# Loads of the dense expert stage moved to ScalarE's queue, its start reordered, and an index row moved to PSUM

## The chip, the cores and the metric

The kernel runs on one core of one Trainium2 chip. The metric is device time in microseconds (us). TensorE (PE in the profile, its weight loads PEld) multiplies matrices into PSUM, VectorE (DVE), ScalarE (ACT) and GpSimd (POOL) compute beside it, and SyncE (SP) issues most DMAs. ACT and POOL issue DMAs too, in the order of their own programs.

## What is computed

The input is 512 tokens of width 1024. A first block mixes gated linear attention with sparse latent attention. Then comes the expert layer, which this change touches, and after it a second block (pooling, stick-breaking attention). The expert layer, cut to what matters:

```python
q = (h @ w_q).reshape(B, S, 8, 256)
s1 = einsum('bshd,nd->bshn', q[..., :128], sub_keys_1)
s2 = einsum('bshd,nd->bshn', q[..., 128:], sub_keys_2)
v1, i1 = top_k(s1, 16);  v2, i2 = top_k(s2, 16)
best, ci = top_k(all 256 sums v1 + v2, 16)
expert_idx = i1[ci // 16] * 128 + i2[ci % 16]      # 128 x 128 experts
gates = softmax(best)
a = gelu(einsum('td,thkd->thk', h, expert_u[expert_idx])) * gates
out = einsum('thk,thkd->td', a, expert_v[expert_idx])
```

## The kernel before, in words

The program is a list of items, each of which issues a few instructions on several engines; every engine then runs its own instructions in that order. All products are float32, made of three passes (L366 to L368): the operands are split into a rounded high part (ACT, L424 for weights) and a rest (mostly POOL, L425). Weights pass through `raw`, which has room for two loads of 1 MB.

**The key stage** (`peer_keys`) finds the 16 experts of each token and head. DVE does most of it. `number` compares a row of the indices 0 to 49 (`c50`, an SBUF row) with the chosen positions (L1322), POOL multiplies by the expert numbers (L1324), DVE sums (L1330). `soft` (L1377 to L1379) makes the gates, `turn` transposes numbers (L1386) and gates (L1387) on PE.

**The table stage** (`peer_table`) builds, for the first 384 tokens, a dense table of gates, expert by token, from small outer products (L1435), and writes it to DRAM (`gates`).

**Hidden products.** For these 384 tokens the layer is computed densely, over all 128 chunks of 128 experts. Chunk c's hidden product is h times its 128 columns of u: 24 matmuls of 384 columns. 72 of the chunks are computed early, in the key and table stages, to keep PE busy there; they are copied out (L1480) and written to DRAM (`hidden`). These chunks are called **spilled** here, and the other 56, computed in the dense stage, **fresh**.

**The dense stage** goes over 32 groups of four chunks. `gate_chunk` takes a chunk: ACT applies GELU (L1519 on the PSUM bank of a fresh chunk, L1516 from the reloaded buffer of a spilled one), DVE multiplies with the gates (L1523, three per chunk), ACT rounds (L1528), DVE subtracts for the rest (L1530). From four chunks, eight **out blocks** of 12 matmuls each (`peer_out`) are made, each of which DVE adds to its accumulator (L1562). A group has four positions, in the order of its chunks 0, 2, 1, 3; usually 0 and 1 are spilled, and 2 and 3 fresh. At each position a chunk is gated, and two out blocks of the group before run on PE. Groups 0, 6, 13, 19 and 26 have four spilled chunks.

In between, the last 128 tokens are computed sparsely: POOL gathers expert rows (L1589), DVE multiplies and adds them (L1617, the dot; L1606, the add), about one per position, and one more in every third group.

The gates of a group (three loads of 256 KB) and the spilled products (192 KB each) are loaded by `fetch_gates`, called by `gate_chunk` with a look-ahead of three chunks, on SP's queue, between the weight loads. A weight load waits until POOL has finished with the `raw` buffer that it takes.

PSUM has eight banks. In the dense stage two pairs hold the sparse rows. Chunks and out blocks take turns through the other four, the ring `out=[0,1,6,7]`, whose banks appear as `bank0_69`, `bank1_70`, `bank6_71` and `bank7_72` below.

The lines of the changed functions follow.

Of the kernel before, what the change touches and what calls it, by code (L numbers as in the profile page):

```python
# [18 lines left out]
P = 128  # L19
# [4 lines left out]
ND = NT - P  # L24
# [6 lines left out]
W = 32  # L31
# [278 lines left out]
class K:  # L310
# [927 lines left out]
    def peer_keys(self):  # L1238

        nc, A = self.nc, self.A  # L1240
# [3 lines left out]
        def keys(u):  # L1244
            A.new_wide("plain")
            A.plain.wake(8 * D)
            self.rows = A.plain.alloc(8 * D, high=False, name="rows")
            self.sk = A.alloc(256, name="sk")
            nc.vector.tensor_copy(self.sk.v(256), u.raw.v(256))
            self.E = A.alloc(NT, name="E")  # L1250
            self.best = A.alloc(NT, name="best")
            self.c50 = A.alloc(64, name="c50")
            nc.gpsimd.iota(self.c50.v(50), pattern=[[1, 50]], base=0, channel_multiplier=0,
                           allow_small_or_imprecise_dtypes=True)

        def ev_q(b, ps):
            s = st[b // 2]
# [60 lines left out]
        def number(h, t):  # L1318

            s = st[h]  # L1320
            eq = A.wide.alloc(800, name="eq")
            nc.vector.tensor_tensor(eq.v(16, 50), self.c50.v(50)[:, None, :].to_broadcast([P, 16, 50]),  # L1322
                                    s["J"].v(TB, 16)[:, t, :, None].to_broadcast([P, 16, 50]), op=OP.is_equal)
            nc.gpsimd.tensor_mul(eq.v(16, 50), eq.v(16, 50), s["X"].v(TB, 50)[:, t, None, :].to_broadcast([P, 16, 50]))  # L1324
            s.setdefault("eq", []).append(eq)
            if t == TB - 1:
                self.free(s["X"], s["J"])
# [5 lines left out]
        items = [Item(keys, [uk], 0.0)]  # L1333
        q = self.blocks("wq", self.t["w_q"], 16, lambda: self.h2, ev_q)
# [34 lines left out]
    def peer_gates(self):  # L1369

        nc, A = self.nc, self.A

        def soft():
            g = self.best.v(32, 16)
            nc.scalar.activation(self.best.v(NT), self.best.v(NT), AF.Exp)
            z = self.tmp(32)
            nc.vector.reduce_sum(z.v(32), g, axis=AX.X)  # L1377
            nc.vector.reciprocal(z.v(32), z.v(32))
            nc.vector.tensor_tensor(g, g, z.v(32)[:, :, None].to_broadcast([P, 32, 16]), op=OP.mult)  # L1379
            self.free(z, self.c50, self.sk)  # L1380

        def turn():
            pe, pg = self.bank("att"), self.bank("att")
            for t in range(TB - 1):
                c = slice(t * P, t * P + P)
                nc.tensor.transpose(pe[:, c], self.E.v(NT)[:, c], self.ident)  # L1386
                nc.tensor.transpose(pg[:, c], self.best.v(NT)[:, c], self.ident)  # L1387
            self.gT, self.iaT, self.ibT = [A.alloc(ND, high=False, name="gT") for _ in range(3)]
            nc.scalar.copy(self.gT.v(ND), pg[:, :ND])
            ei, e2 = self.tmp(ND), self.tmp(ND)  # L1390
            nc.vector.tensor_copy(ei.v(ND, dt=I32), pe[:, :ND])
            nc.vector.tensor_scalar(e2.v(ND, dt=I32), ei.v(ND, dt=I32), P - 1, None, op0=OP.bitwise_and)
# [12 lines left out]

    def peer_table(self, first, fill):
# [43 lines left out]
        items = []  # L1450
        lag = 4
        for n in range(ND // 4 + lag):
            def fn(n=n):
                if n >= lag:
                    outer(n - lag)
                if n < ND // 4:
                    quad(n)
            items.append(Item(fn, (), 0.9))
            if n == lag - 1:
                items += first  # L1460
            if n >= lag and (n - lag) % 4 == 3 and n < ND // 4:
                items += fill[:1]
                del fill[:1]
        return items + fill

    def peer_hidden(self, chunks, spill):

        nc = self.nc
        items = []
        for c0 in chunks[::2]:  # L1470
            u = Unit(self.t["u"][c0 // 2], 2 * D, uses=2, name="u")
            for j in range(2):
                def fn(w, c=c0 + j, j=j):
                    ps = self.bank("hid" if spill else "out")[:, :ND]
                    for k in range(KB):
                        s = slice(j * D + k * P, j * D + k * P + P)
                        self.mm3(ps, (w.hi[:, s], w.lo[:, s]), (self.h2.hi[:, k, slice(ND)], self.h2.lo[:, k, slice(ND)]), k == 0, k == KB - 1)
                    if spill:
                        g = self.rows.v(ND, at=6 * D + self.spilled[c] % 5 * ND)
                        nc.scalar.copy(g, ps)  # L1480
                        self.load(self.H[self.spilled[c]], g, nc.scalar)
                    else:
                        self.gate_chunk(c, ps)
                    if c == P - 1:
                        self.h2.free()
                items.append(Item(fn, [u], 5.3))
        return items

    def fetch_gates(self, upto):

        while self.q_next < min((upto + 3) // 4, P // 4):
            c = 4 * self.q_next
            slots = [self.A.slot("plain", NT, "gates") for _ in range(3)]
            for q, b in enumerate(slots):
                n = P // W
                self.load(b.v(n, 4 * W), self.G[:, n * q:n * q + n, c:c + 4].rearrange("p g b t -> p g (b t)"))
            self.g_slots[self.q_next] = [slots, 4]
            self.q_next += 1
        while self.g_next < min(upto, P):
            c = self.order[self.g_next]  # L1500
            hb = None
            if c in self.spilled:
                hb = self.tmp(ND)
                self.load(hb.v(ND), self.H[self.spilled[c]])
            self.g_bufs[c] = hb
            self.g_next += 1

    def gate_chunk(self, c, ps=None):

        nc = self.nc  # L1510
        i = self.order.index(c)
        self.fetch_gates(i + 3)
        hb = self.g_bufs.pop(c)
        if ps is None:
            ps = self.bank("out")[:, :ND]
# [124 lines left out]
    def peer(self, table, late):  # L1640
# [6 lines left out]
        self.spilled = {c: i for i, c in enumerate(ahead)}  # L1647
        self.order = []
        for gi in range(groups):
            self.order += [4 * gi + i for i in ((0, 2, 1, 3) if gi else range(4))]  # L1650
        rows = self.dram.tile([P, P * ND + 1024], F32, name="gates")
        self.G = rows[:, :P * ND].rearrange("p (g b t) -> p g b t", b=P, t=W)
        self.H = self.dram.tile([len(ahead), P, ND], F32, name="hidden")
# [8 lines left out]
        def reload():  # L1662
            self.x2 = FRows(self, KB, name="x2", slots=True)
            for i in range(KB):
# [6 lines left out]
        items += turn + self.peer_table(hid[n1 - 2:n1], hid[n1:])  # L1671
        end = len(items) - 5
        items[end:end] = [self.rings_at(hid=[6, 7], out=[0, 1, 6, 7]), Item(self.rows_banks, (), 0.0),
                          Item(lambda: self.fetch_gates(5), (), 0.0)]
        items.append(Item(begin, (), 0.0))
        rest = dict(zip(fresh, self.peer_hidden(fresh, False)))
        items.append(rest[6])
        for c in range(3):
            items.append(Item(lambda c=c: (self.gate_chunk(c), self.lowers()), (), 0.0))
        sparse = self.peer_rows()  # L1680
        out = self.peer_out()
        pend = []
        for gi in range(groups):
# [5 lines left out]
            for i in range(4):  # L1689
                c = self.order[4 * gi + i]  # L1690
                n = 1 if gi else 0
                now, sparse = sparse[:n], sparse[n:]
                add, dot = [a for a, _ in now], [b for _, b in now]
                mine = [rest[c] if c in rest else Item(lambda c=c: self.gate_chunk(c), (), 0.0)] if c > 2 and c != 6 else []
                items += add + mine if c in rest else mine + add
                items += (dot or [Item(self.lowers, (), 0.0)]) + pend[2 * i:2 * i + 2]
                if i == 1 and gi and gi % 3 == 0:
                    items += sparse[0]
                    sparse = sparse[1:]
# [422 lines left out]
    def build(self):  # L2122
# [22 lines left out]
        seq.append(self.split_by(nc.vector))  # L2145
        seq.append(self.rings_at(proj=[0, 1, 2, 3], att=[4, 5, 6, 7], hid=[4, 5], out=[0, 1, 2, 3], misc=[6]))
        seq += self.merge()
        seq.append(self.rings_at(proj=[0, 1], att=[2, 3, 4, 5], hid=[6, 7], out=[0, 1, 2, 3]))
        seq.append(self.split_by(nc.gpsimd))
        seq += self.peer(28, 6)  # L2150
        pool = self.pool()
        seq += pool[:2] + [self.split_by(nc.gpsimd)] + pool[2:]
        seq += self.stick()
# [91 lines left out]
```

## Time and profile before

| what | value |
|---|---|
| median of 3 runs | 2877.93 us (2876.39 to 2881.17) |
| the profiled execution | 2877.26 us, span 2875.5 us |
| PE busy | 2700.3 us, 94% of the span |
| DVE, POOL, ACT busy | 64%, 56%, 44% |
| mean granted TensorE clock | 0.978 |

Read the table as averages over stages with different limits. The profile counts a matmul as busy until its modelled end, so the idle time before a matmul and the granted clock of a stretch say more than the share. A granted clock of 1.00 is 2.4 GHz; in the stretches below 1.00 it was at 1.2 GHz for a part of the time. In a row of a timeline, the bracket at the end holds the idle time before the instruction and what ended it.

### The profile page before, as it was taken

The page shows a single profiled execution, that of the slowest core. Times are in us where ns is not written, and L with a number is a line of the kernel's source. Part 1 is how long each engine was busy: PE and PEld are TensorE (multiplying, and loading weights), DVE is VectorE, ACT ScalarE, POOL GpSimd, SP SyncE. Part 2 cuts the span into 40 slices and gives each one's busy share as a digit, 9 for nine tenths or more (in the row PEclk, how much of TensorE's full clock was granted, in tenths as well). Part 3 has the DMA queues.
Part 4 walks back from the last instruction along what each step waited for, and adds up shares of the span by engine and source line. Part 5 has one row for each costly group of instructions (what it writes and reads, how often), then busy time and mean ns, then how long its engine had stood idle before and what let it go on. Part 6 is the DMA issues. An engine that isn't in the chain of part 4 may idle for free.

```text
span 2875.5 us, 40315 instructions
## 1 busy us (share of the span) xinstructions
PE 2700.3 (94%) x14510; PEld 2434.8 (85%) x14510; DVE 1843.2 (64%) x3826; ACT 1254.6 (44%) x2508; POOL 1605.2 (56%) x1481
## 2 busy tenths in 40 slices
PE   5999999898999899898998989989999999999997
PEld 3897788776999899898998989989888887888896
DVE  7334576677888888377767776776585532544655
ACT  4443525523333376444443443444443234445543
POOL 4000234304888765466766766767655554766774
PEclk9999999999999899999999999999999999999998
DMA  6221221265443456598898999888323232221210
GB/s 231 103 74 59 77 89 41 90 227 183 146 142 130 182 227 237 207 334 328 318 333 316 339 330 330 328 321 300 124 87 117 88 103 74 74 74 59 74 59 30
DMA packets 138649, 502.21 MB, mean 175 GB/s; under 512 B 11472, under 2 KB 79184, under 8 KB 89296
## 3 DMA queue, kind: packets, MB, share of 16 engines
q1 hardware_dynamic: 106272, 321.81, 32.8%
q0 software_dynamic: 19072, 136.32, 11.6%
q10 hardware_dynamic: 13104, 41.49, 3.6%
q8 instruction: 114, 1.87, 0.3%
q14 instruction: 87, 0.71, 0.1%
HBM read 456.06 MB, written 43.52 MB: 174 GB/s over the span
## 4 chain that ended last, share of the span: by engine, by line
PE 36%; DVE 7%; DMA 7%; issue 3%; ACT 3%; POOL 3%; SPq 1%; DVEq 0%; POOLq 0%; ACTq 0%
PE bank L366 12%; PE bank L367 11%; PE bank L368 11%; DMA slot<-hidden 5%; POOL split L425 2%; DVE bank L1606 2%; DMA plain<-in_uv_dram,slot 2%; DVE bank L1523 1%; DVE plain L1617 1%; PE bank L2020 1%; DVE slot L1562 1%; PE bank L2019 1%; SPq L376 1%; ACT split L424 1%; ACT bank L1516 0%
## 5 line engine op out<-in xcount | busy, mean ns | idle before, releaser
L425 POOL TENSOR_TENSOR split<-raw,split 128x512 fp32r<-128x512 f32 x832 | 1074.2, 1325 | 637.0 <-ACT split L424 579.0
L366 PE MATMUL bank<-slot,split 128*128 128x384 f32 (+2 forms) x1932 | 706.6, 366 | 16.4 <-DVE slot L373 5.1
L367 PE MATMUL bank<-slot,split 128*128 128x384 f32 (+2 forms) x1932 | 700.8, 363 | 0.5 <-DVE slot L373 0.5
L368 PE MATMUL bank<-slot,split 128*128 128x384 f32 (+2 forms) x1932 | 700.2, 362 | 0.3 <-POOL split L425 0.3
L366 PE MATMUL bank<-wide,split 128*128 128x384 f32 (+1 forms) x1688 | 621.6, 368 | 80.8 <-DVE wide L1530 56.7
L367 PE MATMUL bank<-wide,split 128*128 128x384 f32 (+1 forms) x1688 | 610.8, 362 | 10.0 <-POOL wide L612 10.0
L368 PE MATMUL bank<-wide,split 128*128 128x384 f32 (+1 forms) x1688 | 609.6, 361 | 0.0
L424 ACT CAST split<-raw 128x512 fp32r<-128x512 f32 x953 | 522.3, 619 | 105.4 <-PE bank L367 60.8
L366 PEld LDWEIGHTS bank<-wide,split 128*128 128x128 f32 x1688 | 323.4, 192 | 130.1 <-DVE wide L1530 70.9
L366 PEld LDWEIGHTS bank<-slot,split 128*128 128x128 f32 (+1 forms) x1932 | 366.1, 189 | 59.9 <-DVE slot L373 6.2
L367 PEld LDWEIGHTS bank<-slot,split 128*128 128x128 f32 (+1 forms) x1932 | 365.8, 189 | 37.2 <-DVE slot L373 1.7
L368 PEld LDWEIGHTS bank<-slot,split 128*128 128x128 f32 (+1 forms) x1932 | 365.4, 189 | 37.5 <-POOL split L425 0.6
L367 PEld LDWEIGHTS bank<-wide,split 128*128 128x128 f32 x1688 | 323.7, 192 | 39.6 <-POOL wide L612 12.5
L368 PEld LDWEIGHTS bank<-wide,split 128*128 128x128 f32 x1688 | 323.2, 191 | 26.3
L1523 DVE TENSOR_TENSOR bank<-bank,slot 128x128 f32<-128x128 f32 x384 | 114.5, 298 | 211.0 <-ACT bank L1516 125.6
L1589 POOL DMA_INDIRECT plain<-in_uv_dram,slot x128 | 121.4, 949 | 130.6 <-DVE bank L1606 103.5
L1617 DVE SCALAR_TENSOR_TENSOR plain<-plain,bank 128x1024 f32<-128x1024 f32 x128 | 155.2, 1213 | 24.4 <-DMA plain<-in_uv_dram,slot 24.4
L1606 DVE SCALAR_TENSOR_TENSOR bank<-plain,slot,bank 128x1024 f32<-128x1024 f32 x127 | 162.5, 1280 | 0.0
L1528 ACT CAST wide<-bank 128x384 fp32r<-128x384 f32 x128 | 61.4, 480 | 212.5 <-DVE bank L1523 209.2
L425 DVE TENSOR_TENSOR split<-raw,split 128x512 fp32r<-128x512 f32 x121 | 82.1, 740 | 98.5 <-ACT split L424 96.5
L1562 DVE TENSOR_TENSOR slot<-slot,bank 128x384 f32<-128x384 f32 x240 | 122.5, 548 | 2.5 <-PE bank L368 2.5
L2007 POOL TENSOR_TENSOR slot<-plain,slot 128x384 fp32r<-128x384 f32 (+3 forms) x125 | 107.6, 891 | 0.4 <-DVE slot L2004 0.4
(355 smaller groups left out, 3835.0 us busy)
## 6 DMA issues: line engine op xcount, KB each, us to landing
raw<-in_u_dram SPq DMA_DIRECT2D x64, 1024.0 KB, 5.0
raw<-in_v_dram SPq DMA_DIRECT2D x64, 1024.0 KB, 5.0
gates<-wide ACTq DMA_DIRECT2D x12, 2048.0 KB, 7.8
slot<-gates SPq DMA_DIRECT2D x96, 256.0 KB, 9.0
plain<-in_w_ada_dram SPq DMA_DIRECT2D x32, 512.0 KB, 6.4
raw<-in_w_pool_dram SPq DMA_DIRECT2D x16, 1024.0 KB, 4.9
hidden<-plain ACTq DMA_DIRECT2D x72, 192.0 KB, 2.9
slot<-hidden SPq DMA_DIRECT2D x72, 192.0 KB, 8.1
```

The lines of the kernel that those rows point to most:

```text
L366: mm(out, lhsT=w[0], rhs=x[0], start=start, stop=False, skip_group_check=True)
L367: mm(out, lhsT=w[0], rhs=x[1], start=False, stop=False, skip_group_check=True)
L368: mm(out, lhsT=w[1], rhs=x[0], start=False, stop=stop, skip_group_check=True)
L424: self.nc.scalar.copy(u.hl.hi[:, c], u.raw.v(u.n)[:, c])
L425: (u.lo or self.lo_engine).tensor_sub(u.hl.lo[:, c], u.raw.v(u.n)[:, c], u.hl.hi[:, c])
L1523: nc.vector.tensor_mul(p, p, b.v(P // W, 4, W)[:, :, c % 4])
L1528: nc.scalar.copy(a.hi, ps)
L1562: nc.vector.tensor_add(acc, acc, ps)
L1589: self.nc.gpsimd.indirect_dma_start(out=self.uvs[k % 4].rearrange("p a b -> p (a b)"), out_offset=None, in_=self.t["uv"], in_offset=bass.I ...
L1606: nc.vector.scalar_tensor_tensor(acc, v, a, acc, op0=OP.mult, op1=OP.add)
L1617: nc.vector.scalar_tensor_tensor(u, u, 1.0, self.hx, op0=OP.mult, op1=OP.mult, accum_out=self.dx.v(P)[:, k:k + 1])
L2007: nc.gpsimd.tensor_sub(out[i].lo, e.v(NT - i * P), out[i].hi)
```

## The change

1. `fetch_gates` issues the loads on ACT's queue, except those of the first two groups of gates and the first four spilled chunks. The look-ahead for chunks is 4 in place of 3; that for the gates stays.
2. The dense stage starts in another order: the hidden product of chunk 6, the first fresh one, is computed into bank 6 as before the rest, but chunks 0 to 3 are gated ahead of it, and group 1 runs in the order 2, 0, 1, 3. From there on the ring is `out=[0,1,7]`.
3. `c50` lies in PSUM, in bank 5 behind the columns that `iota` uses later; the ring of the key stage gives up that bank.
4. Two hidden products more stand in the key stage, and two fewer in the table stage (26 in place of 28, two of the 23 places of the table are skipped).

```diff
+            c = self.tmp(50)
+            nc.gpsimd.iota(c.v(50), ...)
+            self.c50 = self.psum[5][:, 256:306]
+            nc.scalar.copy(self.c50, c.v(50))
...
-            if n >= lag and (n - lag) % 4 == 3 and n < ND // 4:
+            if n >= lag and (n - lag) % 4 == 3 and n < ND // 4 and n - lag not in (27, 59):
...
+                    elif c == 6:
+                        self.early = ps
...
-        while self.q_next < min((upto + 3) // 4, P // 4):
+        while self.q_next < min((upto + 2) // 4, P // 4):
...
-                self.load(b.v(n, 4 * W), self.G[...])
+                self.load(b.v(n, 4 * W), self.G[...], nc.scalar if self.q_next > 1 else nc.sync)
...
-                self.load(hb.v(ND), self.H[self.spilled[c]])
+                self.load(hb.v(ND), self.H[self.spilled[c]], nc.scalar if self.g_next > 4 else nc.sync)
...
-        self.fetch_gates(i + 3)
+        self.fetch_gates(i + 4)
...
-            self.order += [4 * gi + i for i in ((0, 2, 1, 3) if gi else range(4))]
+            self.order += [4 * gi + i for i in ((0, 2, 1, 3) if gi > 1 else (2, 0, 1, 3) if gi else range(4))]
...
-        items.append(rest[6])
-        for c in range(3):
+        items += [self.rings_at(out=[6]), rest[6], self.rings_at(out=[0, 1, 7])]
+        for c in range(4):
             items.append(Item(lambda c=c: (self.gate_chunk(c), self.lowers()), (), 0.0))
+        items.append(Item(lambda: (self.gate_chunk(6, self.early), self.lowers()), (), 0.0))
...
-        seq.append(self.rings_at(proj=[0, 1], att=[2, 3, 4, 5], hid=[6, 7], out=[0, 1, 2, 3]))
+        seq.append(self.rings_at(proj=[0, 1], att=[2, 3, 4], hid=[6, 7]))
...
-        seq += self.peer(28, 6)
+        seq += self.peer(26, 6)
```

ACT's program in a group in the middle of the dense stage, before: GELU and rounding of a fresh chunk, two small instructions of the sparse rows, the rounding of weights, and GELU of a spilled chunk.

```order
L1519 ACTIVATE bank7_72<-bank7_72 128x384
L1528 CAST wide694_9365<-bank7_72 128x384
L1613 ACTIVATE slot500_7521<-slot500_7521 128x1
L1614 ACTIVATE slot500_7521<-slot500_7521 128x1
L424 CAST split_66<-raw_65 128x512 x4
L1516 ACTIVATE bank6_71<-slot783_12520 128x384
L1528 CAST wide694_9365<-bank6_71 128x384
```

The same place in the changed kernel, down to the next fresh chunk (its lines 1526, 1535, 1620, 1621 and 1523 are 1519, 1528, 1613, 1614 and 1516 of before):

```order
L1526 ACTIVATE bank0_69<-bank0_69 128x384
L1535 CAST wide694_9366<-bank0_69 128x384
L1620 ACTIVATE slot500_7583<-slot500_7583 128x1
L1621 ACTIVATE slot500_7583<-slot500_7583 128x1
L424 CAST split_66<-raw_65 128x512 x4
L376 DMA slot785_12641<-gates_133 128x4x128
L376 DMA slot786_12642<-gates_133 128x4x128
L376 DMA slot787_12643<-gates_133 128x4x128
L1523 ACTIVATE bank0_69<-slot783_12484 128x384
L1535 CAST wide694_9366<-bank0_69 128x384
...
L376 DMA slot788_12709<-hidden_134 128x384
L1526 ACTIVATE bank0_69<-bank0_69 128x384
```

Once per group three issues of gates stand ahead of the GELU of a spilled chunk; the issue of a spilled product stands ahead of the GELU of a fresh one. All chunks are now gated in bank 0.

DVE's program from the last multiplication of one fresh chunk to the next additions, before; the banks show which of the four each product took.

```order
L1530 TENSOR_TENSOR wide694_9365<-bank7_72,wide694_9365 128x384
L1617 SCALAR_TENSOR_TENSOR plain_67,slot500_7521<-plain_67,bank1024_2_9370 128x1024
L1562 TENSOR_TENSOR slot708_9552<-slot708_9552,bank0_69 128x384
L1562 TENSOR_TENSOR slot709_9553<-slot709_9553,bank1_70 128x384
...
L1530 TENSOR_TENSOR wide694_9365<-bank6_71,wide694_9365 128x384
L1562 TENSOR_TENSOR slot710_9554<-slot710_9554,bank7_72 128x384
L1562 TENSOR_TENSOR slot711_9555<-slot711_9555,bank0_69 128x384
```

The same rows in the changed kernel (1537, 1624 and 1569 are 1530, 1617 and 1562 of before):

```order
L1537 TENSOR_TENSOR wide694_9366<-bank0_69,wide694_9366 128x384
L1624 SCALAR_TENSOR_TENSOR plain_67,slot500_7583<-plain_67,bank1024_2_9371 128x1024
L1569 TENSOR_TENSOR slot708_9553<-slot708_9553,bank1_70 128x384
L1569 TENSOR_TENSOR slot709_9554<-slot709_9554,bank7_72 128x384
...
L1537 TENSOR_TENSOR wide694_9366<-bank0_69,wide694_9366 128x384
L1569 TENSOR_TENSOR slot710_9555<-slot710_9555,bank1_70 128x384
L1569 TENSOR_TENSOR slot711_9556<-slot711_9556,bank7_72 128x384
```

The out blocks take turns in two banks now, 1 and 7, and every chunk stands in bank 0. The order of DVE's instructions is the same.

## Rows read from the trace of the kernel before

**Rows 1.** Stretches: length; busy us (instructions) of PE, PEld, DVE, ACT, POOL; clock; DMA.

```profile
1341.00:1373.00 32.00, 25.21 (x126) 24.25 (x127) 26.23 (x49) 13.62 (x35) 17.86 (x16) 0.89 0.94 351
...
1517.00:1561.00 44.00, 34.66 (x173) 33.38 (x173) 31.04 (x59) 16.28 (x40) 25.64 (x23) 0.88 0.93 347
...
1677.00:1718.00 41.00, 33.34 (x177) 32.06 (x176) 29.32 (x58) 16.37 (x41) 22.62 (x21) 0.92 0.95 349
...
1866.00:1908.00 42.00, 34.33 (x174) 33.69 (x173) 27.96 (x55) 16.29 (x40) 25.23 (x22) 0.88 0.94 339
...
1206.00:1992.00 786.00, 730.15 (x4039) 712.68 (x4039) 566.87 (x1088) 333.27 (x825) 536.68 (x458) 0.97 0.88 322
```

**Rows 2.** Waits from 1206 to 1992: total us, times, longest us.

```profile
ACT bank L1516 <- DMA slot<-hidden: 131.9, 32, 6.0
...
PE bank L366 <- DVE wide L1530: 47.7, 38, 5.4
...
DVE plain L1617 <- DMA plain<-in_uv_dram,slot: 24.4, 19, 2.4
```

**Rows 3.** Timeline, group 13: SP's issues, ACT's GELU, PE's wait.

```profile
1516.17 2.05 SPq L376 DMA_DIRECT2D slot<-gates  x3
1518.26 5.63 SPq L376 DMA_DIRECT2D slot<-hidden  x2
...
1529.05 0.49 ACT L1516 ACTIVATE bank<-slot 128x384 f32<-128x384 f32 x1 [4.70 <-DMA slot<-hidden]
...
1532.25 0.69 PE L366 MATMUL bank<-wide,split 128*128 128x384 f32 x1 [4.13 <-DVE wide L1530]
```

**Rows 4.** Timeline of DVE in a half group without a late load.

```profile
1564.79 1.03 DVE L1562 TENSOR_TENSOR slot<-slot,bank 128x384 f32<-128x384 f32 x2
1566.20 0.97 DVE L1523 TENSOR_TENSOR bank<-bank,slot 128x128 f32<-128x128 f32 x3 [0.38 <-ACT bank L1516]
...
1568.27 0.55 DVE L1530 TENSOR_TENSOR wide<-bank,wide 128x384 fp32r<-128x384 f32 x1
...
1569.87 1.01 DVE L1562 TENSOR_TENSOR slot<-slot,bank 128x384 f32<-128x384 f32 x2
```

**Rows 5.** Same half group: first out-block matmuls, GELU of the spilled chunk.

```profile
1560.91 0.33 PE L366 MATMUL bank<-wide,split 128*128 128x384 f32 x1
...
1565.68 0.49 ACT L1516 ACTIVATE bank<-slot 128x384 f32<-128x384 f32 x1
...
1573.39 0.33 PE L366 MATMUL bank<-wide,split 128*128 128x384 f32 x1
```

**Rows 6.** DMA issues by tile: ns min/median/max, first and last start.

```profile
L376 SPq DMA_DIRECT2D slot<-gates x96: 360/531/2537, 1168.6 to 1997.1; - x96
...
L376 ACTq DMA_DIRECT2D hidden<-plain x72: 326/326/353, 697.1 to 1191.9; - x72
L376 SPq DMA_DIRECT2D slot<-hidden x72: 319/645/8310, 1183.5 to 1981.1; - x72
```

**Rows 7.** DMA from 1206 to 1992: KB each, median us from issue to landing.

```profile
slot<-gates SPq DMA_DIRECT2D x87, 256.0 KB, 9.1
slot<-hidden SPq DMA_DIRECT2D x66, 192.0 KB, 8.2
```

**Rows 8.** Timeline, start of the dense stage.

```profile
1203.93 0.56 DVE L1530 TENSOR_TENSOR wide<-bank,wide 128x384 fp32r<-128x384 f32 x1 [0.60 <-ACT wide L1528]
...
1204.55 0.69 PE L366 MATMUL bank<-wide,split 128*128 128x384 f32 x1 [9.05 <-DVE wide L1530]
```

**Rows 9.** Turn from keys to table: PE's waits.

```profile
963.73 0.47 PE L1386 MATMUL bank<-plain,slot 128*128 128x128 f32 x1 [3.15 <-DVE slot L1330]
...
969.21 0.45 PE L1387 MATMUL bank<-plain,slot 128*128 128x128 f32 x1 [5.01 <-DVE slot L1379]
```

**Rows 10.** DVE comparisons: index row in SBUF (L1322), in PSUM (L1414); ns min/median/max.

```profile
L1322 DVE TENSOR_TENSOR wide<-plain,slot x32: 977/1535/2556, 728.0 to 960.3; 128x800 f32<-128x800 f32 x32
...
L1414 DVE TENSOR_TENSOR slot<-bank,slot x96: 675/681/692, 981.4 to 1156.0; 128x512 f32<-128x512 f32 x96
```

More of the change, by code (lines that the diff above doesn't have):

```diff
@@ L1251, in keys @@
             self.best = A.alloc(NT, name="best")
-            self.c50 = A.alloc(64, name="c50")
-            nc.gpsimd.iota(self.c50.v(50), pattern=[[1, 50]], base=0, channel_multiplier=0,
+            c = self.tmp(50)
+            nc.gpsimd.iota(c.v(50), pattern=[[1, 50]], base=0, channel_multiplier=0,
                            allow_small_or_imprecise_dtypes=True)
+            self.c50 = self.psum[5][:, 256:306]
+            nc.scalar.copy(self.c50, c.v(50))
+            self.free(c)
         def ev_q(b, ps):
@@ L1321, in number @@
             eq = A.wide.alloc(800, name="eq")
-            nc.vector.tensor_tensor(eq.v(16, 50), self.c50.v(50)[:, None, :].to_broadcast([P, 16, 50]),
+            nc.vector.tensor_tensor(eq.v(16, 50), self.c50[:, None, :].to_broadcast([P, 16, 50]),
                                     s["J"].v(TB, 16)[:, t, :, None].to_broadcast([P, 16, 50]), op=OP.is_equal)
@@ L1379, in soft @@
             nc.vector.tensor_tensor(g, g, z.v(32)[:, :, None].to_broadcast([P, 32, 16]), op=OP.mult)
-            self.free(z, self.c50, self.sk)
+            self.free(z, self.sk)
         def turn():
@@ L1489, in fetch_gates @@
     def fetch_gates(self, upto):
-        while self.q_next < min((upto + 3) // 4, P // 4):
+        nc = self.nc
+        while self.q_next < min((upto + 2) // 4, P // 4):
             c = 4 * self.q_next
@@ L1495, in fetch_gates @@
                 n = P // W
-                self.load(b.v(n, 4 * W), self.G[:, n * q:n * q + n, c:c + 4].rearrange("p g b t -> p g (b t)"))
+                self.load(b.v(n, 4 * W), self.G[:, n * q:n * q + n, c:c + 4].rearrange("p g b t -> p g (b t)"),
+                          nc.scalar if self.q_next > 1 else nc.sync)
             self.g_slots[self.q_next] = [slots, 4]
@@ L1673, in peer @@
         items[end:end] = [self.rings_at(hid=[6, 7], out=[0, 1, 6, 7]), Item(self.rows_banks, (), 0.0),
-                          Item(lambda: self.fetch_gates(5), (), 0.0)]
+                          Item(lambda: self.fetch_gates(6), (), 0.0)]
         items.append(Item(begin, (), 0.0))
         rest = dict(zip(fresh, self.peer_hidden(fresh, False)))
-        items.append(rest[6])
-        for c in range(3):
+        items += [self.rings_at(out=[6]), rest[6], self.rings_at(out=[0, 1, 7])]
+        for c in range(4):
             items.append(Item(lambda c=c: (self.gate_chunk(c), self.lowers()), (), 0.0))
+        items.append(Item(lambda: (self.gate_chunk(6, self.early), self.lowers()), (), 0.0))
         sparse = self.peer_rows()
@@ L1693, in peer @@
                 add, dot = [a for a, _ in now], [b for _, b in now]
-                mine = [rest[c] if c in rest else Item(lambda c=c: self.gate_chunk(c), (), 0.0)] if c > 2 and c != 6 else []
+                mine = [rest[c] if c in rest else Item(lambda c=c: self.gate_chunk(c), (), 0.0)] if c > 3 and c != 6 else []
                 items += add + mine if c in rest else mine + add
```

## The prediction

> **What bounds the kernel now.** I read four views, in this order. The waits of the dense stage come first: the longest sum is ACT's, 131.9 us in 32 places, for reloaded spilled products, and PE waits 47.7 us in 38 places for the rest that DVE makes of gated chunks [rows 2]. Then the busy time of stretches: from 1206 to 1992 us PE works 730.15 of 786.00 us, so 55.85 us are idle. The groups with four spilled chunks (6, 13, 19, 26) hold much of it: 159 us with 127.54 busy, so 31.5 us idle, and a clock of 0.88 to 0.92. Length times what is missing to 1.00 (32 x 0.11 + 44 x 0.12 + 41 x 0.08 + 42 x 0.12) gives 17.1 us for the clock, together 48.6 us [rows 1]. The rest of the stage has 24.4 us idle. Then the timeline of group 13 for the cause: SP's issue of three gates takes 2.05 us, that of two spilled products is held for 5.63 us, ACT waits 4.70 us for one of them, and 2.7 us after its GELU ends PE waits 4.13 us [rows 3]. SP issues them between weight loads, each of which waits for its buffer. Last, a half group without a late load: its first out-block matmul stands at 1560.91, the next at 1573.39, 12.48 us for 72 matmuls, 0.173 us each; 24 (a hidden product, or two out blocks) take 4.16 [rows 5]. All times below count from that 1560.91.
>
> **The loads on ACT's queue.** ACT has no weight loads, and the look-ahead is a chunk longer. A position takes 12.48/2 = 6.24 us, so an issue four positions ahead leads by some 25 us less the place inside it; I take 18 to 20. The median landings, 8.2 us for spilled products and 9.1 for gates, fit in [rows 7]. What is then late in a group of four spilled chunks is DVE: from the first multiplication (1566.20) to the end of the additions (1569.87 + 1.01) it needs 4.68 us per spilled position [rows 4], PE's two out blocks 4.16. About 7 positions by 0.52 are 3.6 us, and with a sparse row more about 4.3 per group, 17 for four; pauses as short as these stand all over the stage at clock 1.00, so I take no clock loss. The term is 17 - 48.6 = -32 us. Its bounds are 0 (loads as late as now) and -48.6.
>
> The Trainium skill speaks against this in "DMA: Bandwidth & Descriptors", section "Issuing engines are not separate DMA queues": all issuers end on the same 16 DMA engines, and another issuer saves only the issuing time. Here the issuing time is what is long: two products held SP for 5.63 us [rows 3]. The DMA share of 0.88 over the stage [rows 1] is what speaks for the rule. By it this term would be 0, which is the fourth rival.
>
> **What the issues cost ACT.** Once per group ACT issues three gates right before the GELU of a spilled chunk. On SP an issue of gates has a median of 0.531 us, at most 2.537; ACT's own issues, writes of 192 KB, took 0.326 [rows 6]. ACT issuing loads is not shown, so three cost x = 1.0 by the one row and 1.6 by the other; the upper end is an ACT that is held as SP is, x = 3 and more. I take 1.6, the row for the same load. Behind the issues wait that GELU, its rounding and the chunk's multiplication. Before, this delay was covered, since the next fresh product went to another bank. Now it waits for bank 0: the rest of the spilled chunk ends at 1568.27 + 0.55 = 1568.82, +7.91 [rows 4]; PE comes to the next fresh product at +8.32 (two times 4.16) [rows 5], or +8.66 with the stall below. The cover is 8.66 - 7.91 = 0.75, the stall x - 0.75 = 0.85, and 25 groups give +21 us (6 at x = 1.0, 56 at x = 3). The issue of a spilled product stands ahead of a fresh chunk's GELU, where ACT waits for PE's product anyway: nothing, unless it is held.
>
> **Three banks in place of four.** Out blocks now alternate between banks 1 and 7. The third block of a half group (nominally at +4.16) waits for the addition of the first, which ends half way through the pair of 1.03 us at 1564.79, at +4.39 [rows 4]. With some 0.1 us until PE starts, that is 0.33 per half group; in about 51 half groups +17 us. Bounds: 0 if DVE comes earlier, since ACT is less late, and 30 if DVE's other work goes first as often as now.
>
> In about nine groups an extra sparse row puts DVE behind; DVE's waits for gathered rows, 24.4 us in 19 places [rows 2], are these. With one bank for all chunks, I put 1.1 us on each, +10 (0 to 20). 21 + 17 + 10 = 48 is what the usual groups idle then; before they idled 24.4, mostly from late loads and the same extra rows. The difference is +24, and the dense stage together is -32 + 24 = -8.
>
> **The turn from keys to table.** PE waits 3.15 us at 963.73 for DVE's sum and 5.01 at 969.21 for the gates [rows 9], 8.16 in all. Two hidden products, 2 x 4.16 = 8.3 us of PE's work, move from the table to the key stage. They stand ahead of these waits, and DVE's chain does not wait for them, so they fill the gaps: -8.2. The comparisons with the index row have a median of 1.535 us from SBUF; comparisons from PSUM with 512 columns take 0.681 [rows 10], scaled to 800 columns 1.06. If all 32 gain 0.5, DVE has 16 us more room there, which helps the same wait and is not counted twice. Where the products were taken out of the table, PE may wait up to 3 us. I take -8 (0 to -10.6: the waits and 2.4 us more if DVE's shorter chain also brings the table's start forward).
>
> **The start.** PE's first out block waits 9.05 us, until 1204.55, for chunk 1's rest, made at 1203.93 [rows 8]. With chunks 0 to 3 gated ahead of chunk 6 the rest that it waits for comes about a chunk earlier, some 2 us: -2 (0 to -5). The longer look-ahead costs nothing here, the first four spilled loads staying on SP.
>
> **The sum.** -8 - 8 - 2 = -18 on the profiled execution, 2877.26 us (the median of the runs is 2877.93, 0.7 more, so it stands for them): 2859.3, and 2860 on the median.
>
> **The rivals.**
> *Cheap issues:* ACT's issue of a load is as short as its issue of a write [rows 6]. The stall is 1.0 - 0.75 = 0.25, 25 groups cost 6 instead of 21, and 2860 - 15 = 2845. For it: ACT's queue has no weight loads in it. Against: gates have more and smaller pieces than those writes.
> *The turn gives nothing back:* the two products are computed, but PE waits as long later, for the table's first operands. 2860 + 8 = 2868. Against: the chain to the gates is DVE's.
> *Slower, ACT is held:* the issue of gates waits in ACT's program as SP's did, up to 2.537 us for one [rows 6], with GELU behind it. Each us more on the triple costs 25 us. The dense gain is gone at x = 1.6 + 8/25 = 1.9, all 18 us at x = 2.3; from about 2.6 the kernel is slower. At x = 3.0 it is 2860 + 35 = 2895. For it: the DMA share of 0.88 [rows 1] and SP's 8.310 us for one issue [rows 6]. Against: the median of 0.531, though it stood between blocked weight loads.
> *The loads come no sooner:* the transfers are late because the DMA engines are full, and another queue does not help. The four special groups keep 48.6 in place of 17: 2860 + 32 = 2892. Against: landings of 8.2 and 9.1 us beside leads of 18 us [rows 7].
>
> **How the numbers follow.** I give the forecast 0.46, cheap issues 0.20, no gain at the turn 0.12, ACT held 0.16, no sooner 0.06. From 0.2% on, 5.8 us, a change can be told from none: faster is below 2872, slower above 2884. Forecast, cheap issues and the turn's rival lie on the faster side with 0.78, but their terms' bounds (three banks +13, extra rows +10) reach the middle, which I put at 0.09. So 0.70 faster, 0.10 the same, 0.20 slower. The likeliest case alone spans 2846 to 2872. The range takes in cheap issues with a little of the special groups' lower bound (2838) and both slower rivals (2895).
>
> **What would show it.** Right: ACT's waits for spilled products fall from 131.9 us to under 20; the special groups' clock is 1.00 and their idle near 4 us each; the waits of 3.15 and 5.01 at the turn are gone; PE has short new waits for the addition into the accumulators, 0.3 us per half group, and for bank 0 once per group, 0.9 us; issues of gates on ACT's queue take 0.5 us. Wrong: issues on ACT over 0.8 us each, or GELU of spilled chunks late by more than 2 us behind them; waits of over 2 us for loads in the special groups; waits at the turn of the same sum, moved on; or gates that land behind their chunk's multiplication, a wait that the profile before does not have.

## The result and the profile after

The changed kernel takes 2910.27 us (median of four runs, 2906.05 to 2916.72), the kernel before 2877.16 beside it: a ratio of 1.0111, 95% interval 1.0091 to 1.0130. It is slower, where 2860 and a faster kernel were forecast, and outside the range. The profiled execution has a span of 2904.3 us, 28.8 more than before.

The line of the page with busy time and share, after:

```profile
PE 2714.2 (93%) x14510; PEld 2439.8 (84%) x14510; DVE 1827.5 (63%) x3826; ACT 1261.0 (43%) x2509; POOL 1588.2 (55%) x1481
```

PE runs as many matmuls as before, so the 28.8 us are pauses of PE, with slower matmuls behind the longest of them. To place them, take from each trace the first out-block matmul after each fresh product and cut the program there:

| us | before | changed |
|---|---|---|
| span's start to the first of the 50 marks | 1225.63 | 1218.99 (-6.6) |
| four special groups, mark to mark | 165.3 | 149.0 (-16.3) |
| the usual half groups, up to the last mark | 594.3 | 643.2 (+48.9) |
| last mark to the span's end | 890.2 | 893.1 (+2.9) |

So the turn and the special groups gained, and the usual half groups lost more than twice as much. The first line would be -11.6 but for 5.0 us that the changed kernel's execution was late before the stage in question: the first matmul of the key stage starts at 703.09, and at 698.11 in the trace before (over all traces of this case, at 698.11 to 705.63). PE's waits from there to the dense stage, after:

```profile
703.09 0.50 PE L366 MATMUL bank<-slot,split 128*128 128x512 f32 x1 [1.56 <-ACT slot L1262]
...
985.86 1.97 PE L1438 MATMUL bank<-slot,slot 128*128 128x128 f32 x8 [3.60 <-DVE slot L1425]
...
989.20 1.01 PE L1438 MATMUL bank<-slot,slot 128*128 128x128 f32 x3 [1.37 <-POOL slot L1422]
...
1197.25 0.69 PE L366 MATMUL bank<-wide,split 128*128 128x384 f32 x1 [6.49 <-DVE wide L1537]
...
1204.94 0.44 PE L366 MATMUL bank<-wide,split 128*128 128x384 f32 x1 [0.92 <-DVE slot L1567]
```

The waits of 3.15 and 5.01 us [rows 9] are gone, and the first out block, which waited 9.05 [rows 8], waits 6.49; at 1204.94 there is a new wait of 0.92 for a bank. At the start of the table PE waits 3.60 and 1.37 us, where it had waited 2.0 and 1.9, so the waits of the turn were not just moved there.

The longest waits of the dense stage, 1206 to 2018 us (total, times, longest):

```profile
ACT bank L1523 <- issue: 53.0, 25, 10.1
...
PE bank L366 <- DVE slot L1569: 41.8, 57, 3.6
DVE plain L1624 <- DMA plain<-in_uv_dram,slot: 35.7, 26, 3.3
...
PE bank L366 <- DVE wide L1537: 28.6, 21, 9.0
```

Of the kernel before, 1206 to 1992 us, the line that belongs to PE's wait for additions:

```profile
PE bank L366 <- DVE slot L1562: 7.5, 6, 1.7
```

ACT's 131.9 us for spilled products [rows 2] are gone: no wait of ACT on `hidden` is left. In their place its GELU of spilled chunks stood 53.0 us behind ACT's own issues, and PE waits 41.8 us in 57 places for additions, where it was 7.5 in 6. A usual half group with an issue of gates, in the changed kernel's timeline, shows how one becomes the other:

```profile
1486.87 1.03 DVE L1569 TENSOR_TENSOR slot<-slot,bank 128x384 f32<-128x384 f32 x2
1487.25 2.83 ACTq L376 DMA_DIRECT2D slot<-gates  x3
...
1487.57 0.41 PE L366 MATMUL bank<-wide,split 128*128 128x384 f32 x1 [0.26 <-DVE slot L1569]
1490.18 0.50 ACT L1523 ACTIVATE bank<-slot 128x384 f32<-128x384 f32 x1 [2.34 <-issue]
...
1493.38 0.45 PE L366 MATMUL bank<-slot,split 128*128 128x384 f32 x1 [1.41 <-DVE wide L1537]
```

The first out block of this half stands at 1482.99. The third waits 0.26 us for the addition of the first, since they share a bank, and starts at +4.58 in place of +4.16. The gates' issues end at 1490.08, and only then comes the GELU of the spilled chunk, at +7.19; in the half group before it, which has no gates to issue, it stands at 1474.63, +4.65 behind 1469.98. Its rest is late by as much, and the fresh product, which needs the same bank 0, waits 1.41. In the 25 usual half groups with gates' issues the fresh products start 34.9 us late in all, in the 21 others 5.1 (by the measure that is defined with the experiments).

An issue that is held ahead of the GELU of a spilled chunk reaches PE almost whole. The timeline of group 12, ACT's queue, ACT and PE:

```profile
1515.94 2.16 ACTq L376 DMA_DIRECT2D slot<-gates  x3
1518.15 8.15 ACTq L376 DMA_DIRECT2D slot<-hidden  x1
1526.35 0.49 ACT L1523 ACTIVATE bank<-slot 128x384 f32<-128x384 f32 x1 [10.11 <-issue]
...
1529.54 0.69 PE L366 MATMUL bank<-slot,split 128*128 128x384 f32 x1 [8.96 <-DVE wide L1537]
```

Behind the three gates one issue took 8.15 us. The GELU stood 10.11 us behind all four, and PE waits 8.96. The fresh product behind this wait takes 7.05 us, to 1536.59, in place of 4.16, since the granted clock is 0.56 there (columns as in [rows 1]):

```profile
1529.50:1536.50 7.00, 6.96 (x24) 6.96 (x25) 3.25 (x5) 0.00 (x0) 0.73 (x1) 0.56 0.58 195
```

Before, a pair of such issues held SP for 5.63 us [rows 3], and no arithmetic stands in SP's program.

The place of a held issue decides what it costs. Five issues of spilled products took 4.2 to 8.2 us. Four of them stand ahead of the GELU of a fresh chunk, for which ACT has to wait for PE's product anyway, and cost little. One of them follows the first half group shown:

```profile
1492.39 5.70 ACTq L376 DMA_DIRECT2D slot<-hidden  x1
1498.13 0.47 ACT L1526 ACTIVATE bank<-bank 128x384 f32<-128x384 f32 x1 [5.46 <-PE bank L368]
```

Only ahead of a special group does an issue of a spilled product stand right behind the three gates, ahead of the GELU of a spilled chunk, because only there is the chunk in the second position of the coming group a spilled one. These four issues took 2.75, 8.15, 0.53 and 2.02 us.

The special groups gained less than forecast. A stretch of each of the four, and what PE waits for in the second (columns as in [rows 1]; then the timeline):

```profile
1342.00:1369.00 27.00, 20.67 (x106) 19.55 (x105) 22.52 (x44) 10.57 (x28) 17.75 (x17) 0.94 1.02 397
1545.00:1571.00 26.00, 21.47 (x106) 20.57 (x105) 20.36 (x41) 10.44 (x26) 16.97 (x16) 0.87 1.01 380
1709.00:1734.00 25.00, 20.56 (x114) 19.33 (x114) 20.90 (x41) 10.61 (x27) 17.20 (x16) 1.00 1.01 389
1902.00:1927.00 25.00, 20.07 (x104) 19.40 (x104) 19.44 (x41) 9.92 (x25) 16.10 (x16) 0.93 1.03 392
```

```profile
1552.01 1.22 DVE L1624 SCALAR_TENSOR_TENSOR plain<-plain,bank 128x1024 f32<-128x1024 f32 x1 [2.85 <-DMA plain<-in_uv_dram,slot]
...
1553.85 0.66 PE L366 MATMUL bank<-wide,split 128*128 128x384 f32 x1 [3.17 <-DVE slot L1569]
```

DVE's program is the reason: the dot of a gathered row (L1624) stands ahead of the additions, the row is 2.85 us late, and PE waits 3.17 us for the addition. In the four groups, mark to mark, DVE waits 14.4 us for such rows and PE 17.3 us for additions. The clock in this stretch is 0.87, no better than before, and below 1.00 in three of the four.

### The profile page after: what moved, and what is told of

It reads as the page before. It is cut to its first block, busy times and chain, and to the rows that moved or that the text cites. A ratio compares the mean times of both kernels' runs of the same rounds, so it can differ in the third digit from the quotient of the medians.

```text
span 2904.3 us, 40314 instructions
## 1 busy us (share of the span) xinstructions
PE 2714.2 (93%) x14510; PEld 2439.8 (84%) x14510; DVE 1827.5 (63%) x3826; ACT 1261.0 (43%) x2509; POOL 1588.2 (55%) x1481
## 4 chain that ended last, share of the span: by engine, by line
PE 67%; DVE 12%; ACT 7%; DMA 6%; issue 3%; POOL 3%; ACTq 2%; SPq 0%; DVEq 0%; POOLq 0%
PE bank L366 21%; PE bank L367 20%; PE bank L368 20%; DMA plain<-in_uv_dram,slot 4%; PE bank L1438 3%; ACT split L424 2%; DVE bank L1530 2%; ACTq L376 2%; POOL split L425 2%; DVE plain L1624 1%; DVE split L425 1%; DVE bank L1613 1%; DMA plain<-in_w_ada_dram 1%; PE bank L2028 1%; DVE plain L672 1%
## 5 line engine op out<-in xcount | busy, mean ns | idle before, releaser
L366 PE MATMUL bank<-wide,split 128*128 128x384 f32 (+1 forms) x1688 | 621.8, 368 | 79.8 <-DVE slot L1569 41.8
L1624 DVE SCALAR_TENSOR_TENSOR plain<-plain,bank 128x1024 f32<-128x1024 f32 x128 | 155.4, 1214 | 35.7 <-DMA plain<-in_uv_dram,slot 35.7
L1526 ACT ACTIVATE bank<-bank 128x384 f32<-128x384 f32 x56 | 26.6, 475 | 262.4 <-PE bank L368 262.4
```

The source lines that it names most:

```text
L366: mm(out, lhsT=w[0], rhs=x[0], start=start, stop=False, skip_group_check=True)
L1624: nc.vector.scalar_tensor_tensor(u, u, 1.0, self.hx, op0=OP.mult, op1=OP.mult, accum_out=self.dx.v(P)[:, k:k + 1])
```

## The experiments

Two measures are used below. *Third block* and *fresh product* are, summed over the 46 usual half groups of a profile, what the third out block starts later than 4.16 us after the first, and what the next fresh product starts later than 4.16 us after that. They are 22.0 and 8.5 us before (the expectation for e1 puts the first at about 25), 35.1 and 40.0 in the changed kernel. Ratios are to the kernel before, run beside each; its medians there were 2877.2 to 2879.4 us.

| kernel | banks of the out ring | loads | look-ahead | turn, start | us | ratio, 95% interval |
|---|---|---|---|---|---|---|
| changed | 3 | ACT | 4 | new, new | 2910.27 | 1.0111 (1.0091 to 1.0130) |
| e1 | 4 | ACT | 4 | new, new | 2853.21 | 0.9910 (0.9882 to 0.9938) |
| e2 | 3 | ACT, gates earlier | 4 | new, new | 2897.18 | 1.0061 (1.0039 to 1.0084) |
| e3 | 4 | ACT, gates earlier | 4 | new, new | 2852.41 | 0.9901 (0.9878 to 0.9924) |
| e4 | 4 | ACT | 4 | old, old | 2850.52 | 0.9899 (0.9872 to 0.9926) |
| e5 | 2 for chunks, 2 for out blocks | ACT | 4 | new, new | 2891.82 | 1.0044 (1.0021 to 1.0066) |
| e6 | 1 for chunks, 3 for out blocks | ACT | 4 | new, new | 2909.34 | 1.0105 (1.0088 to 1.0122) |
| e7 | 4 | SP | 4 | old, old | 2843.51 | 0.9875 (0.9859 to 0.9892) |
| e8 | 4 | ACT | 4 | new, old | 2840.17 | 0.9875 (0.9855 to 0.9895) |
| e9 | 4 | SP | 4 | new, old | 2827.27 | 0.9824 (0.9809 to 0.9839) |
| e10 | 3 | SP | 4 | new, new | 2867.88 | 0.9968 (0.9955 to 0.9981) |
| e11 | 4 | SP | 3 | new, old | 2868.05 | 0.9960 (0.9947 to 0.9974) |
| e12 | 4 | SP | 4 | new, new | 2828.58 | 0.9834 (0.9818 to 0.9850) |

**e1, four banks from the start on.** In the changed kernel:

```diff
         items.append(Item(lambda: (self.gate_chunk(6, self.early), self.lowers()), (), 0.0))
+        items.append(self.rings_at(out=[0, 1, 6, 7]))
```

> The changed kernel with one line more: after the first fresh chunk is gated the ring is out=[0,1,6,7] again. Theory of the banks (the loss comes from chunks sharing bank 0 and out blocks sharing two banks): the waits of the usual half groups, 35.1 us at the third out block and 40.0 at the next fresh product in the changed kernel, fall back to about 25 and 9; the special groups stay about 16 us better than before; about 2866 us, 40 less than the changed kernel. Theory of the queue (ACT's issues delay its GELU, and that is the loss in any ring): at least half of the loss stays, 2885 us or more.

2853.21 us, 57 below the changed kernel. Its waits from 1206 to 2010 us:

```profile
ACT bank L1523 <- issue: 53.3, 29, 4.6
DVE plain L1624 <- DMA plain<-in_uv_dram,slot: 53.0, 36, 3.6
...
PE bank L366 <- DVE slot L1569: 21.0, 14, 2.5
PE bank L366 <- DVE wide L1537: 19.4, 20, 2.4
```

ACT's GELU stands behind its issues for as long as before the edit (53.3 against 53.0 us), and PE's waits for DVE fall from 70.4 (41.8 + 28.6) to 40.4. The third block's sum is 8.0, the fresh product's 16.4. So the same delay of ACT costs PE far less with four banks in turn, and the theory of the queue in its strict form (half of the loss in any ring) falls. What the issues still cost there, e12 shows.

**e2 and e3, the gates one position earlier,** with three banks and with four:

```diff
-        while self.q_next < min((upto + 2) // 4, P // 4):
+        while self.q_next < min((upto + 3) // 4, P // 4):
```

> The changed kernel (three banks) with the gates of a group issued one position earlier, ahead of the GELU of a fresh chunk, for which ACT waits anyway. Theory of the banks: the third block's 0.42 us per half group stays (20 us in all), the wait of the fresh product for bank 0 loses its part from the three issues, some 20 us: 2890. Theory that held issues (single ones of 5 to 8 us) or late landings make the loss: no more than 5 us better, 2905.

> Both edits: four banks and the earlier issue of gates. Theory of the banks: with four banks the delay of a spilled chunk's GELU is covered, so the earlier issue gives less than 3 us more: 2863 to 2867. Theory of the queue: the earlier issue is what counts, 15 us or more below the kernel that has only the four banks.

e2 is 13 us better than the changed kernel, not 20; e3 is level with e1, as the theory of the banks had it. The profiled execution of e2 is the longest of its six, 2908.74 us, and shows no gain. In it the fresh product's sum halves, to 19.4, but the third block's rises to 48.5. The waits of e2, 1206 to 2010:

```profile
PE bank L366 <- DVE slot L1569: 52.7, 52, 4.8
DVE plain L1624 <- DMA plain<-in_uv_dram,slot: 52.3, 34, 4.3
```

DVE now waits 52.3 us for gathered rows, 17 more than in the changed kernel, and the additions stand behind its dots. In this execution the gain was turned into a later wait. Why rows land later (a median of 9.8 us against 8.8 from 1206 to 1950 us) was not tried.

**e4, the moved loads alone,** in the kernel before (both conditions, and the look-ahead of four):

```diff
+                          self.nc.scalar if self.q_next > 1 else self.nc.sync)
...
+                self.load(hb.v(ND), self.H[self.spilled[c]], self.nc.scalar if self.g_next > 4 else self.nc.sync)
...
-        self.fetch_gates(i + 3)
+        self.fetch_gates(i + 4)
```

> The kernel before with only the loads moved (ACT's queue, look-ahead of four chunks); four banks, start, index row and hidden products as before. Theory of the banks: the special groups gain some 16 us, the usual half groups lose nothing, so 2860 to 2866. Theory of the queue: slower than before, 2885 or more. If the moved loads gain nothing by themselves: 2877.

2850.52 us, faster than forecast by either theory: 29 us better than before, without the new start, turn and ring.

**e5 and e6, the two sharings apart.** After the first fresh chunk:

```diff
+        items.append(self.rings_at(out=[1, 7, 0, 1, 7, 6]))           # e5
+        items.append(self.rings_at(out=[1, 6, 0, 7, 1, 0, 6, 7, 0]))  # e6
```

> The changed kernel with chunks taking turns in banks 0 and 6 and the out blocks still in banks 1 and 7 (ring [1,7,0,1,7,6] after the start). Theory of the banks, in its two parts: the fresh product's wait falls from 40.0 us in the usual half groups to about 12, the third block's stays near 35: 2880 (30 less than the changed kernel). If the shared out banks make most of the loss: 2900 or more. If two banks for chunks do as much as the four in turn: 2855.

> The changed kernel with the chunks still all in bank 0 and the out blocks taking turns in banks 1, 6 and 7. Theory of the banks: the third block's wait falls from 35.1 us to about 8 as with four banks, the fresh product's wait for bank 0 stays at 35 to 40, somewhat larger since PE comes to it earlier by 0.42 us: 2885 to 2890. If the shared bank of the chunks makes most of the loss, it is 2890 or more; if the shared out banks do, 2865.

e5 gives 18 us of the 57, e6 nothing. The half groups say why. In e5 the fresh product's sum falls from 40.0 to 16.9, but the third block's rises from 35.1 to 41.7. In e6 the third block's falls to 0.0, and the fresh product's rises to 74.3, as much as both had been (75.1). e6's waits, 1206 to 2010:

```profile
PE bank L366 <- DVE wide L1537: 67.5, 34, 10.0
ACT bank L1523 <- issue: 55.4, 23, 9.9
```

The two waits are in series on one chain: a pause at the third block gives the chunk in bank 0 time, and where that pause goes PE is as much earlier at bank 0. A third bank for the out blocks alone gains nothing; a second bank for the chunks alone gains a third of what four banks in turn do.

**e7, the look-ahead alone, loads on SP.** In the kernel before, only `fetch_gates(i + 4)` (with `upto + 2`, so that the gates stay where they are, and 6 in place of 5 at the start).

> The kernel before with the look-ahead of four chunks alone, the loads still on SP's queue. If the queue makes the gain of the moved loads (29 us in the experiment with the loads alone): the spilled products stay late, since their issue waits behind weight loads, 2872 to 2878. If the longer look-ahead makes it: 2850 to 2857.

2843.51 us: the rival. Two of its waits from 1206 to 1960 us, and the issues of spilled products:

```profile
DVE bank L1523 <- DMA slot<-gates: 73.1, 80, 2.9
...
ACT bank L1516 <- DMA slot<-hidden: 2.3, 2, 2.1
```

```profile
L376 SPq DMA_DIRECT2D slot<-hidden x72: 320/650/6066, 1189.2 to 1938.8; - x72
```

SP's issues are held as before, up to 6.07 us, and yet ACT's wait for them falls from 131.9 to 2.3 us. One position more of lead covers the holding. The queue was not what had to change. The gates, whose lead is as before, are what comes late now: DVE waits 73.1 us for them, a wait that the dense stage of the trace before does not have. In the usual half groups PE hardly feels it: the third block's sum is 8.4, the fresh product's 4.8.

**e8 and e11, the turn alone,** with ACT's loads (e8) and in the kernel before (e11); the index row, the two table places and 26 in place of 28, as in the diff of the change.

> The kernel before with the loads on ACT's queue and, beside it, the index row in PSUM and two hidden products moved ahead of the turn; start and four banks as before. If the turn's gain is real (the waits of 3.15 and 5.01 us go): 2842, 8 to 9 below the kernel with the loads alone. If it is given back later: 2850.

> The kernel before with only the index row in PSUM and the two hidden products moved ahead of the turn. The prediction's term: PE's waits of 3.15 and 5.01 us go, 2869, a ratio of 0.997. If it is given back: 2877.

e11 has 0.9960, 11 us of 2879; e8 is 10 below e4, by the ratios 7, with intervals that overlap. From the key stage's first matmul to the first mark e11 takes 517.0 us, the kernel before 527.5, the changed kernel 515.9. The three traces with the old turn (before, e4, e7) all have 527.4 or 527.5 us there, the eleven with the new one 513.8 to 518.2, whichever start they have.

**e9, e10 and e12, the loads back on SP's queue:** e9 is e7 with the turn; e10 the changed kernel, three banks and all, with

```diff
-                          nc.scalar if self.q_next > 1 else nc.sync)
...
-                self.load(hb.v(ND), self.H[self.spilled[c]], nc.scalar if self.g_next > 4 else nc.sync)
+                self.load(hb.v(ND), self.H[self.spilled[c]])
```

and e12 is e10 with the four banks of e1.

> The kernel before with the look-ahead of four chunks, all loads on SP's queue, the index row in PSUM and the two hidden products ahead of the turn. If the turn's gain of 8 to 10 us adds to that of the look-ahead: 2834 (the look-ahead alone had 2843.5). If what is won at the turn is lost again later: 2843.

> The changed kernel, three banks and all, with the loads back on SP's queue (look-ahead of four kept). If ACT's issues are what delays the chain in bank 0: the fresh product's wait falls from 40.0 us to 12 or less in the usual half groups, the third block's stays at 25 to 35: 2880 (30 less than the changed kernel). If the shared bank alone makes the loss: no more than 8 us less, 2902 or more.

> The changed kernel with four banks after the start and the loads on SP's queue: what is left of the change is the look-ahead, the turn and the new start. If all three gains add: 2831, 2 to 3 below the kernel without the new start. If the start gives nothing: 2834.

e10 is 42 us below the changed kernel, and even faster than the kernel before. Its waits, 1206 to 2010:

```profile
PE bank L366 <- DVE slot L1568: 32.4, 55, 4.9
DVE plain L1623 <- DMA plain<-in_uv_dram,slot: 26.6, 21, 2.7
PE bank L366 <- DVE wide L1536: 12.2, 16, 1.3
...
ACT bank L1522 <- DMA slot<-hidden: 4.5, 2, 3.0
```

No wait of ACT behind issues is left. PE's short waits for the shared out banks are still there (55 of them, where the changed kernel had 57), and those for the chunk's bank shrink from 28.6 to 12.2. The third block's sum is 25.6, as expected; the fresh product's is 18.1, where 12 or less was expected. e9 and e12 are the fastest kernels of this study, 0.9824 and 0.9834: the look-ahead and the turn add up (35 and 11 us alone, 52 together in e9), and the new start adds nothing to them.

Four of these traces and the one of the kernel before, one execution each, give the usual half groups by ring and queue. The last column is what the 46 of them take beyond 12.48 us each; *rest* is what of it lies behind the start of the fresh product.

| us | third block | fresh product | rest | sum |
|---|---|---|---|---|
| before: four banks, SP, look-ahead 3 | 22.0 | 8.5 | 3.1 | 33.6 |
| e12: four banks, SP, look-ahead 4 | 8.9 | 4.5 | 0.0 | 13.4 |
| e1: four banks, ACT, look-ahead 4 | 8.0 | 16.4 | 3.7 | 28.1 |
| e10: three banks, SP, look-ahead 4 | 25.6 | 18.1 | 2.2 | 45.9 |
| changed: three banks, ACT, look-ahead 4 | 35.1 | 40.0 | 8.8 | 83.9 |

In these half groups earlier loads gain 20.2 us, three banks cost 32.5, and ACT's issues cost 14.7 with four banks and 38.0 with three.

## Why the prediction was wrong

**Loads moved: right that they were late, wrong in what cures it.** I read SP's held issue as a reason to leave SP. It was enough to issue earlier: e7 gains 35 us with the loads on SP, e4 29 on ACT. The intervals of these two overlap; with the turn beside them (e9 and e8, 0.9824 and 0.9875) SP is the better one clear of the intervals. The rule of the Trainium skill that I had set against the change ("DMA: Bandwidth & Descriptors", section "Issuing engines are not separate DMA queues") says that another issuer saves only issuing time. The runs agree so far: with the look-ahead of four the other issuer (e4) gained no more than the same one (e7), and with the same one 129.6 of ACT's 131.9 us of waiting went. My rival drawn from it, loads as late as before, was wrong: with one position more of lead the spilled products came in time from either queue.

**ACT's issues: the step that failed.** I priced 21 us: x = 1.6 us for three gates, 0.75 covered, 25 groups, and nothing for anything else. The runs show 38.0 (e10 against the changed kernel). The price of the gates was right. On ACT their issue has a median of 0.538 us, where SP's had 0.531 [rows 6], and the three together took some 1.85. The issues by tile, after:

```profile
L376 ACTq DMA_DIRECT2D slot<-gates x90: 367/538/1675, 1209.3 to 2017.2; - x90
...
L376 ACTq DMA_DIRECT2D slot<-hidden x68: 326/338/8152, 1165.1 to 1992.7; - x68
```

The cover was right as well: in the half group shown above the GELU stood 2.34 us behind the issues and the fresh product came 1.66 us late, 1.6 more than in the clean ones, so some 0.75 was covered. In the 22 half groups with gates' issues alone, or with the short one of 0.53 behind them, the changed kernel takes 13.2 us more than e10, 0.6 each where I had 0.85.

What failed is the sentence that the issue of a spilled product stands ahead of a fresh chunk's GELU and costs nothing. Ahead of each special group one stands behind the gates, ahead of a spilled chunk's GELU, and three of these four were held for 2.0 to 8.2 us. Those three half groups take 20.9 us more than in e10, 6.0 of it in the rest, where the clock is lower behind the pause. The sentence that the delay was covered with four banks failed too: there the issues cost 14.7 us. Of the 16.4 us of e1's fresh product 15.5 lie in half groups without gates' issues, most of them where DVE's dot waits for a gathered row and the additions stand behind it. From 1206 to 2010 us DVE waits 53.0 us for rows in e1; in e12, the same ring with the loads on SP:

```profile
DVE plain L1623 <- DMA plain<-in_uv_dram,slot: 33.9, 24, 3.6
```

Why it waits longer for rows when ACT issues the loads is open; no run took this apart. For the whole kernel the issues cost 42 us with three banks (e10 against the changed kernel) and 25 with four (e12 against e1). The rival "ACT is held" had the place and the chain, but it priced a longer triple of gates. At the measured 1.85 my sum would have given 2866. The sign that I had named, GELU more than 2 us behind the issues, came on average (53.0 us in 25 places).

**Three banks: right in size by itself.** I put 0.33 us on each half group; 0.42 stands there (the third block at +4.58 for +4.16), 19 us over 46 half groups, 17 forecast over 51. With the extra rows I had 27 for the usual half groups, and 32.5 is there with the loads on SP. That this wait and the one for bank 0 are one chain was in the sum (+8.66 for +8.32), and e6 shows it. What I missed is that four banks also covered the late issues and rows: going back to four is worth 57 us with the loads on ACT (e1), 39 with them on SP (e12 against e10).

**The usual half groups as a sum.** 48 - 24.4 = +24 was forecast, +48.9 came over the 45 between marks, +50.3 over all 46. That is 32.5 for the banks (27 forecast), 38.0 for the issues (21) and -20.2 for loads in time (-24.4, all that these groups idled). The issues are the term that was mis-sized most.

**The special groups: half.** -32 forecast, -16.3 measured, and -19.6 in e7, where ACT hardly waits for spilled products (145.7 us, mark to mark). Here the step that failed is the next limit: I took DVE's arithmetic, 4.68 us per position, and no clock loss. The runs show loads that DVE waits for. In the changed kernel it is gathered rows, 14.4 us in these groups; the additions stand behind them, PE pauses 17.3 us for these, and the clock is below 1.00 in three of the four stretches. In e7 it is 20.4 us for gates in these groups. Which of the two would be left with both in time was not tried.

**Turn and start.** -8 at the turn, -10.5 in the trace of e11 up to the first mark and 11 in its median, at the edge of the bounds. -2 for the start, nothing measured: e12 and e9 differ by 1.3 us within their intervals. PE's wait of 9.05 us became 6.49, with a new one of 0.92 and one of 1.3 on bank 0 behind it.

**The sum.** Turn and start -10 forecast for -11.6 measured (from the key stage's first matmul on), special -32 for -16.3, usual +24 for +48.9, and +2.9 behind the dense stage, where I had nothing. The sign came from two errors of 16 and 25 us in the same direction, in terms larger than their difference. I gave slower kernels 0.20, although the bounds of the two terms, 0 to -48.6 and 6 to 56 for the issues alone, allowed it easily.

## What to carry to other kernels

Where a load is late because its issue is held, first issue it earlier on the same queue; a queue of an engine that computes makes the issue's time, and above all a held issue, a delay of the arithmetic behind it. Buffers that look idle in a clean stretch are the cover for such delays: before a ring is shortened, work out how late the producer may be. Go through the places that differ from the usual one as well: here three half groups of 46 made more than half of what the issues cost. When a sum is the difference of a large gain and a large loss, its sign is only as good as the worse of the two.

## What the runs showed of the hardware

A comparison with the index row in PSUM took 0.976 us each of 32 times, where it had ranged from 0.977 to 2.556 from SBUF [rows 10], while POOL worked beside it in both:

```profile
L1325 DVE TENSOR_TENSOR wide<-bank,slot x32: 972/976/984, 733.0 to 964.0; 128x800 f32<-128x800 f32 x32
```

PSUM was not faster; it took away the lengthening. The prediction had scaled to 1.06 us. The Trainium skill states a rule for this in "SBUF — State Buffer", section "Who interferes with whom": a VectorE instruction with two SBUF inputs contends with a GpSimd instruction that reads SBUF. The minimum is the same in both places and the spread is gone with one input in PSUM, which agrees.

An issue of a load on ACT's queue can be held as one on SP's, up to 8.15 us, though no weight load stands in ACT's program. While ACT was held at 1518.15 SP issued a weight load in 0.33 us:

```profile
1519.39 0.33 SPq L376 DMA_DIRECT2D raw<-in_v_dram  x1
```

So it is not all issues that stop at such a time. What holds one was not tried.
